# Output weights loaded together, the spectra's groups finished in steps, and the context's norm at the end of its stage

## The chip, the cores and the metric

The kernel runs on one core of a Trainium2 chip. Its time is the device time of one execution in microseconds, and a kernel's time is the median of its runs. Engines are PE (TensorE: matmuls and transposes), DVE (VectorE), ACT (ScalarE), POOL (GpSimd) and SP (SyncE, which issues nearly all transfers here). A transfer is issued by an instruction on SP, which first waits for whatever its buffer waits for; what stands behind it on SP waits as well.

## The reference, cut to what matters

Two layers over 1024 latent tokens of width 1024, with 256 context tokens ahead of them. Layer 0 is attention, layer 1 a recurrence beside a long convolution whose filters come out of a small network. All of it is f32; the kernel splits each f32 operand into a high and a low part and makes a product of three matmuls.

```python
def attn_layer(...):                     # layer 0
    ...
    y = jnp.concatenate([o_a * silu(ga), o_b * silu(gb)], axis=-1) @ w_out
    x = x + gate[:, None] * y
    if ctx_out:
        yc = jnp.concatenate([oa_c * silu(ga_c), ob_c * silu(gb_c)], axis=-1) @ w_out
        ctx = ctx + gate_c * yc

def rec_layer(...):                      # layer 1
    u = modulate(x, norm_g, shift[:, None], scale[:, None]) @ w_in
    uc = modulate(ctx, norm_g, shift_c, scale_c) @ w_in
    ...
    y_hy = hyena_operator(u_hy, hy_short, hyena_filters(...), hy_skip)

def modulate(x, gain, shift, scale):
    return rms_norm(x, gain) * (1 + scale) + shift

def fft_long_conv(z, kern, skip):
    kf = jnp.fft.rfft(kern, n=2 * L, axis=0)      # the filters' spectra
    ...
```

## The kernel before

**Order.** The program is written once, stage after stage, and a scheduler with a timeline model of its own then orders the instructions of each engine. Within `attention` PE is kept in the order of the program; the other engines are the scheduler's. So where an instruction stands on DVE, ACT, POOL and SP is not told by the source; the section on the change shows rows of that order.

**Attention (to 1083 us).** 80 units of two heads by 128 queries: 40 of dense attention (`units_b`), then 40 of `units_a`, four head pairs j with two context units and eight window units (ty, gi) each. `mix` weaves the scores of a unit with the transposes (`pt_ps`) and the output product of the unit before, and calls `next(self.fill)` between them: other work on PE, a slice at a time. A window unit takes the minimum of scores plus bias on DVE (`pn`, L700, L890), the exponentials on ACT (L695), and its bias from POOL (L881) out of a mask and a table (`namask`, `tt`), both loaded for it.

**The spectra (643 to 990 us)** are the first such fill: `hyena_kernels` makes 80 steps, for each of 4 filter blocks (half, o) eight steps of values and two transforms `dft` of six steps. A transform ends with four groups g: a combine (L1805, DVE for g = 0 and 3, POOL for 1 and 2), a multiply by the norm (L1806, DVE), the skip term (L1902, POOL) and the store to `HS` on SP. The tile `hs` has two buffers, and all four groups stand in the program right behind the last step.

**The output weights (990 to 1046 us).** At unit (2, 0, 3) `load_wo` loads `attn_w_out` in eight blocks of 512 KB through two raw tiles; each half block is cast on ACT (`wo_hi`, L192) and its rest taken on POOL (`wo_lo`, L196). From unit (3, 0, 1) the fill is `context_rows`: the output product of the context's two tiles (`c_ps`), whose first input is the load `m` (L957), cast to `m0h`.

**The output product (1083 to 1207 us).** `gemm2` first norms the two context tiles (rows of the modulation `mod` and the gain loaded there, L970 to L973; `norm_mod` L329 to L347: mean square on ACT, scale L339 on DVE, shift L340 on POOL except for tile 9, eight transposes `nm_ps`, a cast and a low part), then takes the latent tiles 2 to 9, 48 matmuls `g_ps` each, gate and residual (L986, L987), store of `X`, and the same norm. Behind it the context is stored (`XC`, L1027), its tiles are given up, and `gemm3` loads its weights `w_raw` (L365), from which ACT casts `w_hi`; `hyena`'s tables `hiv`, `hfw` and `hs` are loaded there too.

## Time and profile before

| | |
|---|---|
| median of 3 runs | 2482.05 us (2478.19 to 2484.31) |
| profiled execution | 2487.22 us, of it the span of the trace 2485.4 us |
| TensorE's granted clock, mean over the span | 0.938 |
| busy share of the span | PE 92%, its weight loads 76%, DVE 63%, ACT 47%, POOL 37% |
| transfers | 362 MB, mean 146 GB/s |
| chain that ended last, by engine | PE 27%, DVE 9%, DMA 3%, issue 2% |

All rows of the trace below are of the profiled execution; times in them are counted from the span's start. The clock's two levels are 1.2 and 2.4 GHz, so a mean of 0.83 in a stretch means that a third of it ran at the lower one.

### The profile page before, as it was taken

Reading aid. Unit: us, or ns where it says so; the run is one execution under the profiler, and the core shown is the slowest. Engines: PE = TensorE matmul, PEld = TensorE weight load, DVE = VectorE, ACT = ScalarE, POOL = GpSimd, SP = SyncE. Lnnn points to the kernel's source line nnn. Section 1 sums busy time; section 2 is a strip of 40 time slices with the busy share of each in tenths; the row PEclk is TensorE's granted clock in tenths of the full one; section 3 lists DMA queues with packets and bytes.
Section 4 is the critical chain, followed back from the end, with each engine's and each line's share of the span. In section 5 each row is a group of like instructions: output and inputs, shape, how many; then the busy total and the mean of one; then the engine's idle time right before and its main releaser. Section 6 shows DMA issues by size and latency. Waiting matters only on the chain. (4 is left out here: it accounts for less than half of the span.)

```text
span 2485.4 us, 45290 instructions
## 1 busy us (share of the span) xinstructions
PE 2275.4 (92%) x16647; PEld 1892.6 (76%) x16647; DVE 1568.8 (63%) x3175; ACT 1177.3 (47%) x2695; POOL 931.4 (37%) x959
## 2 busy tenths in 40 slices
PE   4999999999999989779899889999968999998997
PEld 3877888777878877668778778788757877887775
DVE  6255532368667867455486696457797776777425
ACT  5354434456556555532323221366435656665334
POOL 1253235201011654511033244224745464655512
PEclk8999999999999989889999999999858989999999
DMA  8433344682222766843454544574534343444522
GB/s 280 132 123 119 126 147 146 196 254 93 80 68 90 200 199 183 225 165 110 144 164 150 164 158 136 173 257 134 155 85 131 107 122 97 115 134 126 168 73 92
DMA packets 351428, 361.69 MB, mean 146 GB/s; under 512 B 83106, under 2 KB 283055, under 8 KB 350438
## 3 DMA queue, kind: packets, MB, share of 16 engines
q1 hardware_dynamic: 341894, 330.34, 43.5%
q10 hardware_dynamic: 9168, 24.25, 3.2%
q0 software_dynamic: 144, 4.19, 0.4%
q8 instruction: 132, 2.16, 0.4%
q14 instruction: 90, 0.74, 0.1%
HBM read 260.07 MB, written 100.10 MB: 145 GB/s over the span
## 5 line engine op out<-in xcount | busy, mean ns | idle before, releaser
L158 PE MATMUL g_ps<-xl,w_hi 128*128 128x512 f32 x1056 | 268.0, 399 | 1.0 <-ACT w_hi L192 1.0
L158 PEld LDWEIGHTS g_ps<-xl,w_hi 128*128 128x128 f32 x1056 | 198.9, 191 | 44.0 <-issue 1.9
L158 PE MATMUL s_ps<-k,q 128*128 128x256 f32 (+1 forms) x704 | 199.9, 381 | 7.6 <-DVE pn L700 4.3
L441 POOL TENSOR_TENSOR al_acc<-al_acc,al_t 128x512 f32<-128x512 f32 x98 | 129.0, 1316 | 185.6 <-ACT al_t L439 155.5
L196 DVE TENSOR_TENSOR w_lo<-w_raw,w_hi 128x256 fp32r<-128x256 f32 (+1 forms) x184 | 131.2, 769 | 86.6 <-PE g_ps L158 45.3
L187 ACT COPY pt<-pt_ps 128x512 f32<-128x512 f32 (+1 forms) x203 | 102.1, 506 | 139.3 <-PE pt_ps L161 133.7
L1586 DVE TENSOR_TENSOR tmp<-L,X 80x112 f32<-80x112 f32 (+25 forms) x279 | 136.4, 489 | 17.8 <-DMA L<-LD 8.9
L1588 DVE TENSOR_TENSOR X<-X,tmp 80x112 f32<-80x112 f32 (+25 forms) x279 | 140.6, 504 | 6.5
L158 PE MATMUL g_ps<-xl,w_lo 128*128 128x512 f32 x528 | 137.8, 395 | 0.0
L161 PE MATMUL pt_ps<-ident,p 128*128 128x128 f32 x704 | 118.1, 283 | 17.7 <-DVE pt L185 7.5
L158 PE MATMUL g_ps<-xhi,w_hi 128*128 128x512 f32 (+1 forms) x528 | 118.2, 366 | 8.9 <-DVE ac_res L283 4.7
L161 PEld LDWEIGHTS pt_ps<-ident,p 128*128 128x128 f32 x704 | 80.8, 141 | 52.9 <-DVE pt L185 14.8
L158 PEld LDWEIGHTS s_ps<-k,q 128*128 128x128 f32 x704 | 109.9, 200 | 14.6 <-DVE p L700 7.1
L695 ACT ACTIVATE p<-p,mn 128x1280 f32<-128x1280 f32 (+1 forms) x96 | 103.4, 1077 | 35.7 <-DVE p L700 35.5
L439 ACT ACTIVATE al_t<-al_w,condT 128x512 f32<-128x512 f32 x98 | 70.8, 722 | 101.7 <-POOL al_acc L441 60.9
L158 PE MATMUL g_ps<-xhi,w_lo 128*128 128x512 f32 (+1 forms) x528 | 118.2, 362 | 0.0
L881 POOL TENSOR_TENSOR bias<-namask,tt 128x384 f32<-128x384 f32 x64 | 67.5, 1055 | 125.9 <-DVE mn L890 52.0
L158 PEld LDWEIGHTS g_ps<-xl,w_lo 128*128 128x128 f32 x528 | 98.2, 188 | 21.1 <-issue 1.4
L158 PE MATMUL g_ps<-xlo,w_hi 128*128 128x512 f32 (+1 forms) x528 | 112.8, 356 | 0.0
L158 PEld LDWEIGHTS g_ps<-xhi,w_hi 128*128 128x128 f32 x528 | 90.0, 194 | 29.5 <-DVE qraw L549 5.4
L158 PE MATMUL g_ps<-AKR,BK 64*128 64x128 f32 (+1 forms) x640 | 91.1, 335 | 22.6 <-DVE AKR L1505 14.8
L158 PEld LDWEIGHTS g_ps<-xhi,w_lo 128*128 128x128 f32 x528 | 89.0, 189 | 18.9 <-issue 5.8
(438 smaller groups left out, 5869.4 us busy)
## 6 DMA issues: line engine op xcount, KB each, us to landing
w_raw<-rec_w_in SPq DMA_DIRECT2D x33, 512.0 KB
hfw<-FW SPq DMA_DIRECT2D x32, 512.0 KB
w_raw<-attn_w_in SPq DMA_DIRECT2D x13, 1024.0 KB
al_w<-rec_ada_w SPq DMA_DIRECT2D x48, 256.0 KB
tt<-TG SPq DMA_DIRECT2D x64, 192.0 KB
kkf<-KK SPq DMA_DIRECT2D x40, 256.0 KB
q<-qb SPq DMA_DIRECT2D x64, 128.0 KB
HS<-hs SPq DMA_DIRECT2D x32, 256.0 KB
```

The lines of the kernel that those rows point to most:

```text
L158: return self.keep(self.pe.matmul(*args, **kw))
L161: return self.keep(self.pe.transpose(*args, **kw))
L187: self.nc.scalar.copy(out=out, in_=in_)
L196: e.tensor_tensor(out=lo, in0=full, in1=hi.bitcast(F32), op=ALU.subtract)
L439: nc.scalar.activation(out=o, in_=wt, func=AF.Copy, scale=self.condT[:, k, ci:ci + 1])
L441: nc.gpsimd.tensor_tensor(out=t, in0=t, in1=o, op=ALU.add)
L695: self.nc.scalar.activation(out=p, in_=p, func=AF.Exp, bias=mn, scale=-1.0, accum_out=rs)
L881: nc.gpsimd.tensor_tensor(out=b, in0=mask, in1=tt, op=ALU.subtract)
L1586: nc.vector.tensor_tensor(out=tv, in0=L[:, s:s + 1, rt].to_broadcast([n, nj, nt]), in1=X[:, rj, s:s + 1].to_broadcast([n, nj, nt]), op=ALU ...
L1588: nc.vector.tensor_tensor(out=X[:, rj, rt], in0=X[:, rj, rt], in1=tv, op=ALU.subtract)
```

## The change

Three stages are rewritten.

1. The spectra: the four combines of a transform stand together at its end, POOL's two first; multiply, skip term and store of the groups go into a list, `self.later`, of which one entry is taken at each later step, the remainder at the end. `hs` has four buffers, `hskip` two.
2. The output weights: eight raw tiles, on buffers of the pool that later holds the tiles of the output product; their loads are issued together at unit (2, 0, 3). One block is split in each unit of (2, 1), in the two context units of j = 3, and in (3, 0, 0) and (3, 0, 1). The weights are sixteen tiles instead of two. ACT's casts are kept in the order of the program. `namask` has three buffers instead of four.
3. `norm_rows` loads the rows of the norm; the latent ones at (3, 0, 0). `gemm2` takes the latent tiles first and the context's norm last, with rows that reuse the buffers of the latent ones.

```diff
@@ attention, units_a
                     for slot in range(2):
                         z = slice(slot * 128, slot * 128 + 128)
+                        if j == 3:
+                            next(split)
...
                     if (j, ty, gi) == (2, 0, 3):
                         for _ in self.fill:
                             pass
-                        self.load_wo(pool)
+                        self.fill = iter(())
+                        split = self.load_wo()
+                        next(split)
+                    elif j == 2 and ty == 1 or (j, ty) == (3, 0) and gi < 2:
+                        next(split)
+                    if (j, ty, gi) == (3, 0, 0):
+                        self.mods0 = self.norm_rows(0)
                     if (j, ty, gi) == (3, 0, 1):
+                        assert next(split, None) is None
                         self.fill = self.context_rows(self.ap)
@@ window_unit
-        mask = pool.tile([128, 384], F32, name="namask", tag="namask", bufs=4)
+        mask = pool.tile([128, 384], F32, name="namask", tag="namask", bufs=3)
@@ load_wo
-        whi = p.tile([128, KT, D], F32R, name="wo_hi")
-        wlo = p.tile([128, KT, D], F32R, name="wo_lo")
+        self.wo = [[p.tile([128, D], F32R, name=f"wo{i}{k}") for k in range(KT)] for i in range(2)]
...
-        with self.tc.tile_pool(name="wo_raw", bufs=1, side="right", reuse_waits="tile") as rp:
-            raws = [rp.tile([128, D], F32, name=f"wo_raw{i}") for i in range(2)]
-            for k in range(KT):
-                raw = raws[k % 2]
-                nc.sync.dma_start(out=raw, in_=a["attn_w_out"][k * 128:(k + 1) * 128, :])
-                for z in (slice(0, 512), slice(512, 1024)):
-                    self.split(whi[:, k, z], wlo[:, k, z], raw[:, z])
-        self.wo = whi, wlo
+        raws = [self.m_pool.tile([128, D], F32, name="wo_raw", tag=t, bufs=1)
+                for t in ("mod1", "mod0", "xt", "mod2", "m0h", "m0l", "x_c0", "x_c1")]
+        for k in range(KT):
+            nc.sync.dma_start(out=raws[k], in_=a["attn_w_out"][k * 128:(k + 1) * 128, :])
+        yield
+        for k in range(KT):
+            hi, lo = self.wo[0][k], self.wo[1][k]
+            for z in (slice(0, 512), slice(512, 1024)):
+                self.tc.keep_in_program_order(nc.scalar.copy(out=hi[:, z], in_=raws[k][:, z]))
+                nc.gpsimd.tensor_tensor(out=lo[:, z], in0=raws[k][:, z], in1=hi[:, z].bitcast(F32), op=ALU.subtract)
+            yield
+
+    def norm_rows(self, ci):
+        nc, p = self.nc, self.m_pool
+        mods = {}
+        for kind in (1, 0):
+            t = mods[kind, ci] = p.tile([128, D], F32, name=f"mod{kind}", tag=f"mod{kind}", bufs=1)
+            nc.sync.dma_start(out=t, in_=self.AD[1][ci, kind * D:kind * D + D].partition_broadcast(128))
+        g = p.tile([128, D], F32, name="gain1", tag="xt", bufs=1)
+        nc.sync.dma_start(out=g, in_=self.a["rec_norm"].partition_broadcast(128))
+        nc.vector.scalar_tensor_tensor(out=mods[1, ci], in0=mods[1, ci], scalar=1.0, in1=g, op0=ALU.add, op1=ALU.mult)
+        return mods
@@ gemm2
-        for ci, tiles in ((1, range(2)), (0, range(2, 10))):
-            mods = {}
-            for kind, l in ((2, 0), (1, 1), (0, 1))[ci:]:
...
-            nc.vector.scalar_tensor_tensor(out=mods[1, ci], in0=mods[1, ci], scalar=1.0, in1=g, op0=ALU.add, op1=ALU.mult)
+        for ci, tiles in ((0, range(2, 10)), (1, range(2))):
+            mods = self.norm_rows(1) if ci else self.mods0
...
@@ dft
-        for g, x, y, op in ((0, "0+", "1+", ALU.add), (3, "0+", "1+", ALU.subtract), (1, "0-", "1-", ALU.add),
-                            (2, "0-", "1-", ALU.subtract)):
-            e = nc.vector if g in (0, 3) else nc.gpsimd
-            t = wp.tile([128, 2, W], F32, name="hs", tag="hs", bufs=2)
-            e.tensor_tensor(out=t, in0=half[x[0], x[1]], in1=half[y[0], y[1]], op=op)
-            nc.vector.tensor_tensor(out=t, in0=t, in1=nrm().unsqueeze(1).to_broadcast([128, 2, W]), op=ALU.mult)
-            put(g, t)
+        ts = {}
+        for g, x, y, op in ((1, "0-", "1-", ALU.add), (2, "0-", "1-", ALU.subtract), (0, "0+", "1+", ALU.add),
+                            (3, "0+", "1+", ALU.subtract)):
+            t = ts[g] = wp.tile([128, 2, W], F32, name="hs", tag="hs", bufs=4)
+            (nc.vector if g in (0, 3) else nc.gpsimd).tensor_tensor(out=t, in0=half[x[0], x[1]], in1=half[y[0], y[1]], op=op)
+
+        def finish(g):
+            nc.vector.tensor_tensor(out=ts[g], in0=ts[g], in1=nrm().unsqueeze(1).to_broadcast([128, 2, W]), op=ALU.mult)
+            put(g, ts[g])
+
+        self.later += [lambda g=g: finish(g) for g in (0, 3, 1, 2)]
@@ hyena_kernels
+        def now():
+            if self.later:
+                self.later.pop(0)()
...
+                        now()
                         yield
...
+            while self.later:
+                now()
```

What the scheduler makes of it, at the three places that the prediction speaks of. The lines are those of the kernel that the rows belong to; the semaphores that an instruction waits for stand in brackets, by the engine or transfer queue that raises them.

VectorE around the end of a transform (the third of eight), before: `d_h` are the transform's last sums, `hs` the groups, `hnrm` the norm; `fin`, `mst`, `ri`, `pn`, `pt` belong to the attention units.

```order
L1798 TENSOR_TENSOR d_h<-d_f,d_ps 128x512 [waits PE_49,Activation_49]
...
L1805 TENSOR_TENSOR hs<-d_h 128x512 [waits DVE_49]
L732 TENSOR_TENSOR fin<-rb_ps,g 128x128 [waits PE_49]
L1805 TENSOR_TENSOR hs<-d_h 128x512
...
L1806 TENSOR_TENSOR hs<-hs,hnrm 128x512 [waits DVE_49]
L733 TENSOR_TENSOR mst<-o_ps,fin 128x128 [waits DVE_49]
L1806 TENSOR_TENSOR hs<-hs,hnrm 128x512 [waits DVE_49]
...
L890 ISA pn,mn<-s_ps,bias,mn 128x384 [waits DVE_49,PE_49]
...
L1806 TENSOR_TENSOR hs<-hs,hnrm 128x512 [waits DMAHW3_49,Pool_49]
...
L890 ISA pn,mn<-s_ps,bias,mn 128x384 [waits DVE_49,PE_49]
...
L1806 TENSOR_TENSOR hs<-hs,hnrm 128x512 [waits DMAHW5_49,Pool_49]
```

The same place in the changed kernel:

```order
L1820 TENSOR_TENSOR d_h<-d_f,d_ps 128x512 [waits PE_49,Activation_49]
L725 RECIPROCAL ri<-rs 128x2 [waits Activation_49]
L1827 TENSOR_TENSOR hs<-d_h 128x512 [waits DMAHW3_49]
L1827 TENSOR_TENSOR hs<-d_h 128x512
L732 TENSOR_TENSOR fin<-rb_ps,g 128x128 [waits DMAHW5_49,PE_49]
L1830 TENSOR_TENSOR hs<-hs,hnrm 128x512 [waits DVE_49]
L1830 TENSOR_TENSOR hs<-hs,hnrm 128x512 [waits Pool_49]
L1830 TENSOR_TENSOR hs<-hs,hnrm 128x512 [waits DVE_49]
...
L733 TENSOR_TENSOR mst<-o_ps,fin 128x8x16 [waits DMAHW2_49,DVE_49]
...
L1830 TENSOR_TENSOR hs<-hs,hnrm 128x512 [waits Pool_49]
```

The two multiplies of POOL's groups stood behind the next step's work; now all four multiplies follow the two combines, and two of them wait for POOL.

SyncE from the first output weights to the context's first `m`, before; `mod_11527` is the context's gate, `x_c` its residual rows, `M` the store of attention's output.

```order
L922 DMA wo_raw_10752<-attn_w_out 128x1024 [waits DMAHW7_49]
L922 DMA wo_raw_10753<-attn_w_out 128x1024 [waits DMAHW0_49]
L846 DMA vw_11263<-VA 32x4x128 [waits DMAHW1_49]
...
L922 DMA wo_raw_10752<-attn_w_out 128x1024 [waits DMAHW5_49,Pool_49]
...
L922 DMA wo_raw_10753<-attn_w_out 128x1024 [waits DMAHW2_49,Pool_49]
...
L922 DMA wo_raw_10752<-attn_w_out 128x1024 [waits DMAHW3_49,Pool_49]
...
L933 DMA mod_11527<-AD_98 128x1024 [waits DMAHW5_49]
L938 DMA x_c_11535<-ctx 128x1024 [waits DMAHW6_49]
...
L922 DMA wo_raw_10753<-attn_w_out 128x1024 [waits DMAHW0_49,Pool_49]
...
L922 DMA wo_raw_10752<-attn_w_out 128x1024 [waits DMAHW7_49,Pool_49]
...
L957 DMA m_11529<-M_96 128x8x128 [waits DMAHW4_49]
...
L922 DMA wo_raw_10753<-attn_w_out 128x1024 [waits DMAHW0_49,Pool_49]
```

The same place in the changed kernel; `mod_11308`, `mod_11310` and `gain` are the latent norm's rows, `mod_11550` the context's gate:

```order
L888 DMA tt<-TG 128x1x384 [waits DMAHW1_49,Pool_49]
L931 DMA wo_raw<-attn_w_out 128x1024 [waits DMAHW2_49]
...
L931 DMA wo_raw<-attn_w_out 128x1024 [waits DMAHW1_49]
L833 DMA M_96<-mst 128x512 [waits DMAHW2_49,DVE_49]
L831 DMA g<-G_67 128x512 [waits DMAHW3_49]
...
L946 DMA mod_11308<-AD_99 128x1024 [waits DMAHW1_49,Pool_49]
...
L946 DMA mod_11310<-AD_99 128x1024 [waits DMAHW2_49,Pool_49]
...
L948 DMA gain_11312<-rec_norm 128x1024 [waits DMAHW4_49,Pool_49]
...
L958 DMA mod_11550<-AD_98 128x1024 [waits DMAHW3_49,Pool_49]
...
L963 DMA x_c_11558<-ctx 128x1024 [waits DMAHW5_49,Pool_49]
...
L963 DMA x_c_11859<-ctx 128x1024 [waits DMAHW1_49,Pool_49]
...
L982 DMA m_11552<-M_96 128x8x128 [waits DMAHW6_49]
```

All eight loads stand in a row (the first and the last are shown), and the load of `m` now has three rows of the norm and both context rows ahead of it, each of which waits for POOL.

SyncE at the end of the output product, before: `hiv`, `hfw` and `hs` are the convolution's tables and spectra. The context's store `XC` had gone out earlier in the stage.

```order
L989 DMA X_97<-xr 128x1024 [waits DMAHW2_49,DVE_49]
L989 DMA X_97<-xr 128x1024 [waits DMAHW6_49,DMAHW4_49,DVE_49]
L365 DMA w_raw<-rec_w_in 128x8x128 x2
L1916 DMA hiv<-k_idft 128x4096 [waits PE_49]
L1925 DMA hfw<-FW 128x1024 x2
L1953 DMA hs<-HS_5058 128x512
```

The same place in the changed kernel:

```order
L1011 DMA X_97<-xr 128x1024 [waits DMAHW0_49,DVE_49]
L946 DMA mod_12779<-AD_99 128x1024 [waits DVE_49]
L946 DMA mod_12781<-AD_99 128x1024 [waits DMAHW4_49,DVE_49,Pool_49]
L1952 DMA hiv<-k_idft 128x4096 [waits DVE_49,PE_49,Activation_49]
L1961 DMA hfw<-FW 128x1024 [waits PE_49]
...
L1989 DMA hs<-HS_5058 128x512
L1049 DMA XC<-xc_12071 128x2048 [waits DMAHW1_49,Activation_49]
L1989 DMA hs<-HS_5058 128x512 [waits DMAHW2_49]
L1049 DMA XC<-xc_12072 128x2048 [waits DMAHW3_49,DVE_49]
...
L365 DMA w_raw<-rec_w_in 128x8x128 [waits DMAHW6_49,DMAHW1_49]
L365 DMA w_raw<-rec_w_in 128x8x128 [waits DMAHW7_49]
```

The rows of the context's norm wait for DVE's last use of the latent ones; the stores of the context stand behind the tables, and the first load of `gemm3`'s weights behind them waits for one of the stores to have landed.

## Rows read from the trace of the kernel before

**Rows 1.** The page's first part: busy time of each engine, its share of the span, and the number of instructions.

```profile
PE 2275.4 (92%) x16647; PEld 1892.6 (76%) x16647; DVE 1568.8 (63%) x3175; ACT 1177.3 (47%) x2695; POOL 931.4 (37%) x959
```

**Rows 2.** Windows (start:end in us from the span's start): length, then busy us and instructions of PE, PE's weight loads, VectorE, ScalarE and GpSimd, then TensorE's granted clock as a share of full speed, the mean busy share of the DMA engines, and GB/s.

```profile
643.00:990.00 347.00, 320.24 (x2880) 278.11 (x2876) 262.12 (x711) 193.08 (x370) 123.50 (x115) 0.96 0.47 137
990.00:1020.00 30.00, 20.38 (x190) 16.49 (x186) 14.68 (x57) 15.48 (x36) 16.79 (x15) 0.87 0.86 237
1020.00:1040.00 20.00, 13.95 (x100) 11.78 (x101) 10.08 (x31) 12.28 (x26) 12.05 (x11) 0.76 0.99 262
990.00:1050.00 60.00, 44.33 (x355) 36.66 (x352) 28.83 (x103) 31.94 (x70) 34.85 (x31) 0.83 0.88 244
1094.00:1114.20 20.20, 7.16 (x27) 4.39 (x25) 15.10 (x18) 4.62 (x9) 8.71 (x6) 0.58 0.65 227
1198.20:1207.10 8.90, 1.95 (x9) 1.58 (x9) 5.79 (x15) 3.32 (x8) 0.00 (x0) 0.78 0.76 219
1207.00:1220.00 13.00, 12.91 (x51) 10.56 (x52) 3.14 (x9) 3.11 (x10) 0.00 (x0) 0.89 1.04 376
```

**Rows 3.** The view of waits, VectorE, 643 to 990 us: what waited for what, us in total, times, the longest.

```profile
DVE hs L1806 <- POOL hs L1805: 9.3, 5, 4.7
```

**Rows 4.** The timeline of VectorE between 886 and 970 us: start, length in us, line, operation, tiles, shapes, count, and in brackets the idle time before it with what ended that.

```profile
891.92 1.73 DVE L1806 TENSOR_TENSOR hs<-hs,hnrm 128x512 f32<-128x512 f32 x1 [4.74 <-POOL hs L1805]
...
894.69 0.69 DVE L1806 TENSOR_TENSOR hs<-hs,hnrm 128x512 f32<-128x512 f32 x1
...
967.04 1.77 DVE L1806 TENSOR_TENSOR hs<-hs,hnrm 128x512 f32<-128x512 f32 x1 [1.82 <-POOL hs L1805]
```

**Rows 5.** The timeline of GpSimd at 890 us, columns as before.

```profile
890.63 2.48 POOL L1805 TENSOR_TENSOR hs<-d_h 128x512 f32<-128x512 f32 x2 [4.91 <-DMA HS<-hs]
```

**Rows 6.** The view of waits, PE, 643 to 990 us.

```profile
PE s_ps L158 <- DVE pn L700: 4.3, 2, 4.0
PE pt_ps L161 <- ACT pn L695: 3.7, 3, 1.8
...
PE s_ps L158 <- DVE p L700: 2.4, 3, 1.8
PE d_ps L158 <- DVE d_h L1798: 2.2, 1, 2.2
```

**Rows 7.** Instructions of one tile or line over the whole span: line, engine, operation, tiles, count, then shortest/median/longest in ns, and the first and last start in us. SPq are the DMA issues on SyncE.

```profile
L196 POOL TENSOR_TENSOR wo_lo<-wo_raw,wo_hi x16: 1267/1274/1302, 999.2 to 1045.1; 128x512 fp32r<-128x512 f32 x16
L922 SPq DMA_DIRECT2D wo_raw<-attn_w_out x8: 333/377/520, 991.2 to 1033.9; - x8
...
L881 POOL TENSOR_TENSOR bias<-namask,tt x64: 992/1010/1466, 514.4 to 1063.0; 128x384 f32<-128x384 f32 x64
...
L973 DVE SCALAR_TENSOR_TENSOR mod<-mod,gain x2: 1208/1216/1224, 1094.8 to 1105.9; 128x1024 f32<-128x1024 f32 x2
...
L340 POOL TENSOR_TENSOR nm_h<-nm_h,mod x18: 1262/1472/1717, 1096.9 to 1192.3; 128x512 f32<-128x512 f32 x18
```

**Rows 8.** The view of waits, ScalarE, 985 to 1046 us.

```profile
ACT wo_hi L192 <- DMA wo_raw<-attn_w_out: 12.8, 6, 4.2
```

**Rows 9.** The view of waits, PE, 985 to 1050 us.

```profile
PE pt_ps L161 <- ACT pn L695: 12.9, 5, 4.7
```

**Rows 10.** The timeline of ScalarE from 996 to 1208 us.

```profile
998.49 1.14 ACT L192 CAST wo_hi<-wo_raw 128x512 fp32r<-128x512 f32 x2 [3.52 <-DMA wo_raw<-attn_w_out]
...
1037.34 1.04 ACT L192 CAST m0h<-m 128x1024 fp32r<-128x1024 f32 x1 [0.86 <-DMA m<-M]
...
1113.12 1.04 ACT L192 CAST m0h<-m 128x1024 fp32r<-128x1024 f32 x1 [5.26 <-DMA m<-M]
...
1136.26 1.05 ACT L192 CAST m0h<-m 128x1024 fp32r<-128x1024 f32 x1 [5.11 <-PE g_ps L158]
...
1171.77 1.05 ACT L192 CAST m0h<-m 128x1024 fp32r<-128x1024 f32 x1 [5.83 <-PE g_ps L158]
...
1206.63 1.63 ACT L192 CAST w_hi<-w_raw 128x256 fp32r<-128x256 f32 x5
```

**Rows 11.** The timeline of PE (matmuls and transposes) from 1036 to 1208 us.

```profile
1038.44 2.08 PE L158 MATMUL c_ps<-wo_hi,m0h 128*128 128x512 f32 x4 [0.88 <-ACT m0h L192]
...
1083.31 2.14 PE L158 MATMUL g_ps<-wo_hi,m0h 128*128 128x512 f32 x8
...
1092.55 1.98 PE L158 MATMUL g_ps<-wo_hi,m0l 128*128 128x512 f32 x8
...
1197.67 0.47 PE L158 MATMUL g_ps<-wo_hi,m0l 128*128 128x512 f32 x1
...
1207.09 1.22 PE L158 MATMUL g_ps<-xl,w_hi 128*128 128x512 f32 x2 [0.98 <-ACT w_hi L192]
```

**Rows 12.** The timeline of SyncE's DMA issues from 1029 to 1201 us.

```profile
1030.26 0.43 SPq L957 DMA_DIRECT2D m<-M  x1
...
1107.16 0.37 SPq L957 DMA_DIRECT2D m<-M  x1
...
1200.55 0.43 SPq L365 DMA_DIRECT2D w_raw<-rec_w_in  x1
```

**Rows 13.** The timeline of VectorE from 1083 to 1203 us.

```profile
1094.76 1.22 DVE L973 SCALAR_TENSOR_TENSOR mod<-mod,gain 128x1024 f32<-128x1024 f32 x1 [4.94 <-DMA gain<-rec_norm]
...
1202.01 1.41 DVE L339 SCALAR_TENSOR_TENSOR nm_h<-xr,nm_rs,mod 128x512 f32<-128x512 f32 x2
```

## What the change was expected to do

> **What bounds the kernel now.** Read the page's totals first, then the windows by stage, and last the waits inside the three stages that the change touches. TensorE is busy for 92% of the span [rows 1], so time can come only out of the holes in its work, and out of the stretches at the lower of its two clock levels (1.2 against 2.4 GHz) that stand beside the holes. The windows [rows 2] show where the holes are. From 643 to 990 us (attention with the filters' spectra woven in) PE is busy 320.24 of 347.00 us. From 990 to 1050, where the output weights come in, it is busy 44.33 of 60 at a clock of 0.83, and the DMA engines are at 0.88. At the opening of the output product, 1094.0 to 1114.2 holds only 7.16 us of PE work at clock 0.58; the end of that stage, 1198.2 to 1207.1, holds 1.95. The four parts of the change aim at these holes, and the last part makes one larger.
>
> **A, the spectra's groups.** What waits on them in 643 to 990: VectorE waited 9.3 us in 5 places for a GpSimd combine [rows 3], the longest 4.74 us, behind a GpSimd that had itself waited 4.91 us for a store of an older group, since only two buffers rotate [rows 4, 5]. PE passed some of it on: waits for pn, p and d_h of 4.3, 3.7, 2.4 and 2.2 us [rows 6], in all 12.6 us. The clock of 0.96 over 347 us [rows 2] means that some 28 us ran at half speed, which costs up to 14 us; the work of those stretches is not all PE's, and I give half of that, 7, to these waits. With four buffers and both GpSimd combines ahead, these waits go: 12.6 + 7 = 19.6 us at most. But the deferral reaches VectorE only in part. The order of the changed kernel (shown ahead) puts the two combines and all four multiplies within twelve instructions, where before two of the multiplies stood some fifteen further on. That is a burst of 6 x 0.69 = 4.1 us at the undisturbed duration, and 0.69 grows to 1.73 and 1.77 when GpSimd works beside it [rows 4], so it is 4 to 10 us long, ahead of the next scores' minima and of their exponentials. A burst that held PE up for 1.5 us in each of the 8 transforms would take back 12. I take -7. Ends: -16 (hardly any burst felt) and +6 (every burst costs PE about 3.2 us, near the 3.7 and 4.3 of [rows 6]).
> VectorE's multiply lasts 1.73 us while GpSimd's combines run and 0.69 just after them [rows 4, 5]. The Trainium skill, SBUF — State Buffer, "Who interferes with whom", states that a VectorE instruction with two SBUF inputs and a GpSimd instruction that reads SBUF contend for one port pair, which one of them holds for its whole length. The trace agrees by that pair of durations, and the rule speaks against this change, which sets the combines of both engines side by side; by it A would be nearer to +6 than to -7.
>
> **B, the output weights.** Before, two raw tiles rotate, so the eight loads go out between 991.2 and 1033.9 [rows 7], each after the split of an older one. ScalarE's casts stand in line with the softmax and wait 12.8 us for the loads, 6 times [rows 8], and PE waits 12.9 us for the pn behind them [rows 9]. Half speed costs up to (1 - 0.83) x 60 = 10 us here [rows 2]. So 23 us at most could come back. After, all eight loads go out together, and one wait remains: two casts stand in the unit after the issue, and a lone wait was 3.52 us [rows 10]. That would give about -18.
> What is late next is the context's product. Its matmul at 1038.44 waited for the cast of m [rows 11], whose load went out at 1030.26 [rows 12] and was waited for until 1037.34 [rows 10]. In the changed order the m load stands behind all eight raw loads, both rows of the latent norm with the gain, and both context rows, and each of those waits in SyncE's line for a GpSimd split (16 x 1.27 us beside biases of 1.01 us [rows 7]). The transfer engines were at 0.86 in 990 to 1020 and at 0.99 in 1020 to 1040, at 262 GB/s [rows 2]. Ahead of m come five more 512 KB pieces than before (the last raw tile, the two norm rows, the gain, the second context row): 5 x 2.0 = 10 us at that rate, 7 at the 376 GB/s that the gemm behind reached [rows 2]. The slack up to 1037 is 30 x 0.14 = 4. So the product may begin 3 to 6 us later than 1038, although the units ahead of it run sooner; nothing behind it can pass it on PE, whose order is the program's. I take 0, between -18 and +22 (the slower rival).
>
> **C, the opening of the output product.** The hole from 1094.0 to 1114.2 goes. Its first stop is the gain: VectorE stood 4.94 us until 1094.76 [rows 13]; then the context's norm goes through GpSimd at 1.47 us a half [rows 7], PE's transposes wait for it, and m of the next tile is late by 5.26 us [rows 10]. In the changed kernel the latent rows and gain are loaded during attention and the latent tiles come first. A tile in the steady part takes (1171.77 - 1136.26) / 3 = 11.84 us [rows 10]. The stage from 1083.31 to 1198.14 [rows 11] is 114.83 us; eight tiles at that pace, the last without another tile's transposes in it (11.2 us, as the first one's six groups of matmuls, 1083.31 to 1094.53 [rows 11]), are 7 x 11.84 + 11.2 = 94.1. So C is -21; ends -24 and -17.
>
> **D, the context's norm at the end.** Let T be the end of the last output matmul, 1198.14. Before, the last latent tile's norm and transposes lie between, and gemm3 begins at 1207.09 [rows 11], T + 9.0; its weights had been issued at 1200.55 [rows 12]. After, the context's rows reuse the buffers of the latent rows, so their loads go out once VectorE has read those for the last time: T + 5.3 (1202.01 + 1.41 [rows 13]). Landing 5 to 6 us, as the cast at 1113.12 waited for a load issued at 1107.16 [rows 10, 12]: T + 11. Scale by the gain, 1.2 us [rows 7], T + 12; first products 0.7, four GpSimd additions at 1.47: T + 18.8; the last transposes, cast and low part, 2 us more: T + 21. Only then can the store of the context leave, and the first weight load stands behind it in SyncE's line and waits until its first half has landed (the order shown ahead). That 1 MB shares the queue with a 2 MB table and 1.25 MB of other loads issued from T + 15: 4.3 MB at 376 GB/s are 11.5 us, so T + 27. Weights issued then need 6 us (1200.55 to 1206.63 [rows 10, 12]): T + 33. Against T + 9.0 that is +24. Ends +17 (store and loads each in 3 us) and +30.
>
> **E, the rest.** From about 1790 us the scheduler orders all engines otherwise, with the same work. I find no row that would give this a sign: 0, with 8 either way. The reduced mask buffers, 4 to 3, cost nothing while biases are made a unit ahead; if that cover fails, a bias of 1.01 us shows in a unit.
>
> **Sum.** -7 + 0 - 21 + 24 + 0 = -4. The profiled execution took 2487.2 us, so 2483.2, and it stood 5.2 above the median of the runs, 2482.05; so I forecast **2478**. A measurement of this kernel can tell about 0.3%, 7.4 us, from no change: the borders are 2474.6 and 2489.5. The forecast is no change that can be told; its own range is 2468 to 2488.
>
> **Rivals.**
> *Faster: the weights' stage runs through.* If the queue at depth moves the loads at 376 GB/s rather than 262, m is there as soon as the shortened units reach it, and B is -18: 2460. For it: the rate of 376 at 1207 to 1220, and 12.9 us of PE waits with one cause. Against it: share 0.99 in 1020 to 1040. Chance 0.25.
> *Slower: m comes late.* Place: SyncE's line in front of the m load; price: all eight raw tiles and the three norm pieces ahead of it instead of two raw tiles in flight, 11 x 2.0 = 22 us at 262 GB/s; it decides when the first context matmul begins after 1050, where the units have nothing left to cover it. 2500. For it: the full transfer engines; against it: much of this was loaded before m already. Chance 0.12.
> The Trainium skill, DMA: Bandwidth & Descriptors, "Queues, rings and completion order", says that each transfer engine takes the descriptors of one queue in the order issued, so that m's could not start ahead of what is in that line. No row here shows it; by the rule this rival would be likelier than I have it.
> *Slower: the bursts.* The multiplies are not spread, so A is +8 rather than -7: 2493. For it: 1.73 against 0.69 us. Against it: the bursts of before had two multiplies side by side and PE's waits were mostly at GpSimd's. Chance 0.13.
> Forecast 0.40; the other 0.10 is the order of the recurrent stage, both ways.
>
> **How the numbers follow.** Faster: 0.24 of the first rival, 0.14 of the forecast's lower part, 0.04 of the rest: 0.42. Slower: 0.11 + 0.09 of the two, 0.04 + 0.04: 0.28. Same: 0.30. The range takes in the first rival with its spread and the bursts, and leaves out most of a late m: 2455 to 2498.
>
> **What would show it.** C: no PE hole behind the first latent tile, last output matmul some 94 us after the first. D: a hole of 20 us or more before gemm3, with PE waiting for w_hi, which waits for a load. B: one ScalarE wait for a raw tile, and first context matmul at 1033 to 1043 (counted as before, less what A gave). A: no VectorE wait for GpSimd's combine over 1 us, but multiplies of over 1 us in a row. It is wrong if the first context matmul moves by over 10 us, if D's hole is under 12, or if the stage behind 1800 changes by over 8.

## The result

The changed kernel takes 2502.59 us (median of 4 runs, 2498.93 to 2507.42), the kernel before 2480.12 (4 runs). The ratio is 1.0091 with a 95% interval of 1.0063 to 1.012: **slower by 0.9%**, outside the forecast range of 2455 to 2498. The profiled execution took 2499.21 us, 12.0 more than the profiled one of before. Cut into stages by marks that both traces have, these 12 us are a sum of large terms of both signs:

| mark in the trace (us from the span's start) | before | changed | step |
|---|---|---|---|
| end of the attention unit under the last spectra | 981.2 | 996.8 | A +15.6 |
| first matmul of the context's product (`c_ps`) | 1038.4 | 1069.3 | B +15.3 |
| first matmul of the output product | 1083.3 | 1114.9 | +0.7 |
| last matmul of the output product | 1198.1 | 1208.7 | C -21.0 |
| first matmul of the projections (`gemm3`) | 1207.1 | 1247.3 | D +29.6 |
| end | 2485.4 | 2497.4 | E -28.2 |

**A.** VectorE in the changed kernel around the end of the third transform (start, length, line, operation, tiles, count, idle time before):

```profile
713.11 0.69 DVE L1820 TENSOR_TENSOR d_h<-d_f,d_ps 128x512 f32<-128x512 f32 x1 [1.01 <-PE d_ps L158]
713.71 2.36 DVE L1827 TENSOR_TENSOR hs<-d_h 128x512 f32<-128x512 f32 x2
716.00 3.49 DVE L1830 TENSOR_TENSOR hs<-hs,hnrm 128x512 f32<-128x512 f32 x3
719.41 0.28 DVE L732 TENSOR_TENSOR fin<-rb_ps,g 128x128 f32<-128x128 f32 x1
719.62 1.01 DVE L1830 TENSOR_TENSOR hs<-hs,hnrm 128x512 f32<-128x512 f32 x1
720.55 0.41 DVE L700 TENSOR_SCALAR_CACHE_REDUCE p<-s_ps 128x256 f32<-128x256 f32 x1
```

The six operations of the burst fill VectorE from 713.7 to 720.6, and the unit's minimum `p` comes only then. PE at that place:

```profile
721.66 1.12 PE L158 MATMUL o_ps<-pt,vb 128*64 128x128 f32 x8 [4.11 <-ACT p L695]
```

The unit with that wait takes 7.6 us where it took 2.9 before; in the unit behind it the kernel before is the slower one (9.7 against 6.4), and a lag of 5.2 us falls to 1.9. So this place shows how a burst acts, not what each costs. No wait for a GpSimd combine is left in this stretch: the waits of [rows 3] are gone, and the bursts cost more than they did. The stretch as a whole, before and changed (columns as in [rows 2]):

```profile
643.00:981.20 338.20, 313.04 (x2817) 272.27 (x2811) 254.16 (x689) 188.78 (x360) 116.06 (x108) 0.96 0.46 135
```

```profile
643.00:996.80 353.80, 317.76 (x2816) 276.67 (x2812) 262.51 (x679) 187.64 (x357) 126.60 (x106) 0.94 0.44 127
```

TensorE's idle time grew from 25.2 to 36.0 us; a second profile of each kernel has 25.0 and 37.0. So 11 to 12 us of A are holes that repeat. The other 5 are busy time at a lower mean clock, and in the second pair that part is -2.

The group rows of VectorE, 643 to 1000 us (busy, mean ns):

```profile
L1830 DVE TENSOR_TENSOR hs<-hs,hnrm 128x512 f32<-128x512 f32 x31 | 32.3, 1081 | 0.0
...
L1827 DVE TENSOR_TENSOR hs<-d_h 128x512 f32<-128x512 f32 x16 | 19.3, 1248 | 0.0
```

**B.** SyncE's issues of the output weights and of the context's loads:

```profile
1008.11 4.34 SPq L931 DMA_DIRECT2D wo_raw<-attn_w_out  x8
...
1053.01 0.38 SPq L963 DMA_DIRECT2D x_c<-ctx  x1
...
1055.45 0.33 SPq L963 DMA_DIRECT2D x_c<-ctx  x1
...
1059.70 0.38 SPq L982 DMA_DIRECT2D m<-M  x1
```

ScalarE and PE at the two ends of this stretch, which answer to [rows 10, 11]:

```profile
1014.02 1.14 ACT L936 CAST wo<-wo_raw 128x512 fp32r<-128x512 f32 x2 [5.41 <-issue]
...
1068.19 1.04 ACT L192 CAST m0h<-m 128x1024 fp32r<-128x1024 f32 x1 [10.00 <-DMA m<-M]
```

```profile
1069.29 2.08 PE L158 MATMUL c_ps<-wo,m0h 128*128 128x512 f32 x4 [12.96 <-ACT m0h L192]
```

Of the repeated waits for raw tiles [rows 8] one idle stretch of 5.4 us is left, as forecast; the view names nothing that ended it ("issue"), and the cast behind it comes 5.9 us after the first load left. But `m` leaves 51.6 us after the first raw tile, where it was 39.0, and PE stands 13 us for it.

**C and D.** Windows of the changed kernel (length, PE, PE's weight loads, VectorE, ScalarE, GpSimd, clock, share of the transfer engines, GB/s):

```profile
1115.00:1130.00 15.00, 15.00 (x66) 12.36 (x67) 6.41 (x10) 2.87 (x3) 0.00 (x0) 1.00 0.72 227
1130.00:1208.70 78.70, 78.70 (x374) 65.00 (x373) 41.05 (x64) 22.81 (x40) 20.33 (x14) 1.00 0.36 121
1208.70:1247.30 38.60, 6.87 (x29) 4.66 (x27) 15.28 (x27) 8.86 (x19) 6.13 (x4) 0.54 0.66 231
```

The output product runs without a hole at full clock, 93.8 us instead of 114.8. Behind it stands a hole of 38.6 instead of 9.0. SyncE and ScalarE in it:

```profile
1214.85 1.56 SPq L946 DMA_DIRECT2D mod<-AD  x2
1225.31 0.33 SPq L1952 DMA_DIRECT2D hiv<-k_idft  x1
...
1229.40 0.32 SPq L1049 DMA_DIRECT2D XC<-xc  x1
...
1240.49 8.63 SPq L365 DMA_DIRECT2D w_raw<-rec_w_in  x3
```

```profile
1246.86 1.32 ACT L192 CAST w_hi<-w_raw 128x256 fp32r<-128x256 f32 x4 [17.48 <-DMA w_raw<-rec_w_in]
```

With T as in the forecast, the end of the last output matmul: rows of the norm at T + 6, context's store at T + 20.7, weights at T + 31.8, their cast at T + 38. That is the chain of the forecast, with 11.1 us instead of 6 between store and weights. From the table's issue to the weights' the transfer engines were full:

```profile
1225.30:1240.50 15.20, 2.77 (x11) 1.57 (x9) 2.70 (x8) 1.76 (x3) 2.28 (x2) 0.50 0.93 338
```

**E.** The scan, from its first state matmul (`st_ps`) to the first matmul of the last projection (`fe_ps`), before and changed:

```profile
1874.10:2280.70 406.60, 385.90 (x4313) 323.79 (x4309) 303.88 (x707) 257.13 (x847) 227.22 (x321) 0.92 0.42 116
```

```profile
1911.50:2297.00 385.50, 373.01 (x4297) 310.37 (x4296) 292.72 (x709) 255.72 (x845) 229.97 (x320) 0.98 0.45 123
```

The same matmuls in another order: the scan is 21.1 of E's 28.2 us. PE's idle time in it fell from 20.7 to 12.5 us, and its busy time by 12.9 as the clock rose from 0.92 to 0.98.

### The profile page after: what moved, and what is told of

Same layout as the page of the kernel before. It is cut to its first block, busy times and chain, and to the rows that moved or that the text cites. A ratio compares the mean times of both kernels' runs of the same rounds, so it can differ in the third digit from the quotient of the medians.

```text
span 2497.4 us, 45285 instructions
## 1 busy us (share of the span) xinstructions
PE 2269.2 (91%) x16647; PEld 1885.8 (76%) x16647; DVE 1563.2 (63%) x3175; ACT 1177.2 (47%) x2695; POOL 945.7 (38%) x959
## 5 line engine op out<-in xcount | busy, mean ns | idle before, releaser
L1608 DVE TENSOR_TENSOR tmp<-L,X 80x112 f32<-80x112 f32 (+28 forms) x279 | 133.5, 478 | 24.8 <-DMA L<-LD 10.9
L1610 DVE TENSOR_TENSOR X<-X,tmp 80x112 f32<-80x112 f32 (+28 forms) x279 | 133.1, 477 | 6.1
L158 PEld LDWEIGHTS s_ps<-k,q 128*128 128x128 f32 x704 | 110.6, 201 | 15.3 <-DVE pn L700 7.9
L695 ACT ACTIVATE p<-p,mn 128x1280 f32<-128x1280 f32 (+1 forms) x96 | 103.4, 1077 | 38.3 <-DVE p L700 37.9
L158 PEld LDWEIGHTS g_ps<-xl,w_lo 128*128 128x128 f32 x528 | 98.3, 188 | 21.1 <-issue 1.4
L192 ACT CAST w_hi<-w_raw 128x256 fp32r<-128x256 f32 (+1 forms) x184 | 72.1, 463 | 77.9 <-PE g_ps L158 58.9
L158 PE MATMUL g_ps<-AKR,BK 64*128 64x128 f32 (+1 forms) x640 | 94.2, 324 | 12.8 <-DVE tmp L1608 7.3
```

The source lines that it names most:

```text
L158: return self.keep(self.pe.matmul(*args, **kw))
L192: nc.scalar.copy(out=hi, in_=full)
L695: self.nc.scalar.activation(out=p, in_=p, func=AF.Exp, bias=mn, scale=-1.0, accum_out=rs)
L1608: nc.vector.tensor_tensor(out=tv, in0=L[:, s:s + 1, rt].to_broadcast([n, nj, nt]), in1=X[:, rj, s:s + 1].to_broadcast([n, nj, nt]), op=ALU ...
L1610: nc.vector.tensor_tensor(out=X[:, rj, rt], in0=X[:, rj, rt], in1=tv, op=ALU.subtract)
```

## The experiments

All marks in one table, from one profiled execution of each kernel: end of the unit under the last spectra; from there to the first context matmul; the output product; from its end to the projections; from there to the end.

| kernel | A: unit | B: to `c_ps` | C: product | D: to `gemm3` | E: rest | median of runs |
|---|---|---|---|---|---|---|
| before | 981.2 | 57.2 | 114.8 | 9.0 | 1278.3 | 2480.1 |
| before_again | 984.1 | 55.5 | 115.7 | 8.9 | 1273.3 | one run |
| changed | 996.8 | 72.5 | 93.8 | 38.6 | 1250.1 | 2502.6 |
| changed_again | 994.0 | 71.6 | 94.4 | 38.4 | 1261.9 | one run |
| undo_spectra | 981.2 | 66.4 | 93.9 | 39.2 | 1253.4 | 2480.3 |
| undo_weights | 997.5 | 68.0 | 93.8 | 34.3 | 1271.6 | 2514.0 |
| context_norm_first | 992.5 | 71.6 | 95.8 | 16.6 | 1282.8 | 2497.8 |
| spread_multiplies | 970.0 | 69.9 | 93.8 | 38.2 | 1259.5 | 2476.2 |
| m_ahead | 993.6 | 66.9 | 93.9 | 38.1 | 1252.1 | 2493.1 |
| store_ahead_of_table | 993.2 | 69.0 | 93.8 | 37.4 | 1246.9 | 2502.1 |
| two_mended | 973.5 | 71.7 | 95.8 | 11.4 | 1270.0 | 2467.9 |
| three_mended | 974.5 | 66.3 | 95.9 | 11.3 | 1257.1 | 2455.4 |
| four_buffers | 976.5 | 60.8 | 114.6 | 9.0 | 1259.9 | 2466.2 |
| combines_on_vector | 988.7 | 71.2 | 93.8 | 38.3 | 1249.2 | one run |

The context's product between B and C took 43.7 to 45.6 us in all of them. The medians come from four sets of runs, in which the kernel before had 2480.1, 2481.7, 2479.9 and 2476.0; a ratio below is to the kernel before of the same set. E moves by up to 36 us from order to order, and a median can follow it rather than the edit: context_norm_first reaches the projections 25.9 us ahead of the changed kernel and has a median only 4.8 lower, and undo_weights is 8.6 ahead there and 11.4 slower. So the stages carry the argument, not the medians.

**undo_spectra**: `dft` and `hyena_kernels` of the kernel before in the changed one.

> The changed kernel with the spectra's groups as they were before (two buffers, each group finished where it is made). Theory 1 (the bursts of combines and multiplies on VectorE cost PE 15 us up to the last of the spectra and some 5 more in the unit behind): the unit that ended at 996.8 us ends at 981 to 984, the first context matmul begins at 1047 to 1052 instead of 1069.3, and the difference of 20 us is still there at the first matmul of the recurrent layer's projections (1227 instead of 1247). Theory 2 (the units are late for another reason, such as the three mask buffers): 994 or later. In the whole time the recurrent stage behind, whose order changes with every edit, may add or take up to 28 us, as it did between the two kernels.

Measured: 981.2, first context matmul 1047.6, projections 1225.8, that is 15.6, 21.7 and 21.5 us earlier than changed. Theory 1 holds in its numbers; the three mask buffers are no cause of A. That the 6 us behind the mark are the last burst's is not shown: eight issues fewer stand ahead of `m` in this run (52), and it leaves 45.8 us after the first raw tile instead of 51.6. 1.0002 (0.9981 to 1.0023) of before.

**undo_weights**

```diff
-        raws = [self.m_pool.tile([128, D], F32, name="wo_raw", tag=t, bufs=1)
-                for t in ("mod1", "mod0", "xt", "mod2", "m0h", "m0l", "x_c0", "x_c1")]
...
+            raw = self.m_pool.tile([128, D], F32, name="wo_raw", tag=("mod2", "x_c1")[k % 2], bufs=1)
```

> The changed kernel with the output weights loaded as before through two raw tiles (on buffers that the context's product needs only later), casts and splits where the scheduler puts them; the rest as changed. Theory 1 (the line of transfers on SyncE moves at one issue per 0.86 us, since each waits for the eighth before it, and m comes as many issues later as stand ahead of it: 60 in the changed kernel, 45 before, 55 here): first raw load to m's issue 47 us instead of 51.6, so the first context matmul some 4 to 6 us earlier, and ScalarE waits for raw tiles again (over 10 us in all). Theory 2 (the eight large loads in a row take the time): the first context matmul 57 to 60 us behind the last spectra's unit (996.8), as before, instead of 72.5, so 12 to 15 us earlier.

Measured: `m` left 47.3 us after the first raw tile, and the stretch from the spectra's unit is 68.0 instead of 72.5. ScalarE waited 12.8 us for raw tiles again. Theory 1, to a us in `m`'s issue; the first context matmul came 3.8 us earlier. The eight loads in a row are at most 4.5 of B's 15.3 us. 1.0162 (1.0111 to 1.0212) of before.

**context_norm_first**

```diff
-                        self.mods0 = self.norm_rows(0)
+                        self.mods0 = self.norm_rows(1)
...
-        for ci, tiles in ((0, range(2, 10)), (1, range(2))):
-            mods = self.norm_rows(1) if ci else self.mods0
+        for ci, tiles in ((1, range(2)), (0, range(2, 10))):
+            mods = self.mods0 if ci else self.norm_rows(0)
```

> The changed kernel with the context's norm first again, but on rows and gain that were loaded during attention, and the latent rows loaded behind it. Theory 1 (the changed order's last link, norm, store, then weights, costs 30 us at the end of the stage; the opening hole was the late gain and rows, not the order): no hole at the opening, last output matmul 93 to 98 us after the first (93.8 changed, 114.8 before), and 8 to 10 us from it to the projections' first matmul instead of 38.6: there 27 to 31 us earlier than the changed kernel. Theory 2 (the context's norm between the tiles makes the opening hole whatever was loaded): 110 to 115 us again, and a gain of 10 to 14 only.

Measured: output product 95.8, so the opening hole was the late rows and not the order. Behind it 16.6, not 8 to 10, because the table `hiv` had taken the place ahead of the weights. SyncE, then ScalarE:

```profile
1207.11 0.42 SPq L1952 DMA_DIRECT2D hiv<-k_idft  x1
1207.59 1.31 SPq L1961 DMA_DIRECT2D hfw<-FW  x2
1208.94 5.49 SPq L365 DMA_DIRECT2D w_raw<-rec_w_in  x2
```

```profile
1220.91 1.32 ACT L192 CAST w_hi<-w_raw 128x256 fp32r<-128x256 f32 x4 [7.61 <-DMA w_raw<-rec_w_in]
```

Weights issued at 1208.94 behind 3 MB are cast 12.0 us later; before, ahead of them, it was 6.1 [rows 10, 12]. 1.0075 (1.0042 to 1.0109) of before.

**spread_multiplies**

```diff
-            nc.vector.tensor_tensor(out=ts[g], in0=ts[g], in1=nrm()...
+            self.tc.keep_in_program_order(nc.vector.tensor_tensor(out=ts[g], in0=ts[g], in1=nrm()...
```

> The changed kernel with the four multiplies of each transform pinned to the place in VectorE's line that the program gives them, one per step, and the combines as changed. Theory 1 (the burst of six is what PE waits for): the unit that ended at 996.8 ends at 978 to 984, at or ahead of the kernel before, since the waits for GpSimd's combines are gone as well. Theory 2 (the combines of VectorE and GpSimd side by side are the cost, each at 1.25 us on VectorE instead of 0.69, and these stay): 990 or later.

Measured: 970.0, better than either bound: 24 to 27 us under the two profiles of the changed kernel and 11 to 14 under those of before. The combines are as slow as in the changed kernel:

```profile
L1830 DVE TENSOR_TENSOR hs<-hs,hnrm 128x512 f32<-128x512 f32 x32 | 30.8, 973 | 0.0
...
L1827 DVE TENSOR_TENSOR hs<-d_h 128x512 f32<-128x512 f32 x16 | 19.3, 1248 | 0.0
```

So the burst was what PE waited for (theory 2 had 990 or later), and the deferral does what it says only where VectorE's order is pinned. 0.9987 (0.9969 to 1.0005) of before, B and D still in it.

**m_ahead**: the load of `m` is written first at (3, 0, 1), and what must stand behind it is pinned.

```diff
+                        self.mc0 = self.load_m(0, self.m_pool)
+                        self.m_ctx = self.m_load
...
+            with self.tc.issue_after(self.m_ctx.ins):
+                nc.sync.dma_start(out=xt, in_=self.xsrc(tt))
```

> The changed kernel with one difference in SyncE's line: the load of the context's first m is written ahead of the masks and tables of the units from (3, 0, 2) on and of the context rows, and these are pinned behind it, so that 47 issues stand between the first raw load and m instead of 60. Theory 1 (the line moves one issue per 0.84 to 0.88 us whatever is in it, as in all six kernels so far): m goes out 40 to 41 us after the first raw load (51.6 in the changed kernel), and the first context matmul comes 8 to 12 us earlier, at 1057 to 1062. Theory 2 (m waits for the context's attention output or for the splits, not for the line): m at 1055 or later and the first context matmul at 1065 to 1070.

Measured: `m` left after 43.4 us, as SyncE first waited for the context's own store (1045.31), and the first context matmul came at 1060.5, 8.8 us earlier; 5.6 of these fall behind the spectra's unit. `m` was cast at 1052.84, though, 8 us ahead of the matmul. PE's one wait from 1048 to 1062:

```profile
PE pt_ps L161 <- ACT pn L695: 10.1, 1, 10.1
```

The tables put behind `m` are now what comes last; GpSimd, which makes the bias out of them, stood for one until 1054.66:

```profile
1054.66 2.28 POOL L895 TENSOR_TENSOR bias<-namask,tt 128x384 f32<-128x384 f32 x2 [11.90 <-DMA tt<-TG]
```

The line gives one transfer its place at another's cost. 1.0052 (1.0033 to 1.007) of before.

**store_ahead_of_table**

```diff
-                    nc.sync.dma_start(out=self.XC[p], in_=self.xc[p].bitcast(F32))
+                    self.xc_store = nc.sync.dma_start(out=self.XC[p], in_=self.xc[p].bitcast(F32))
...
+        with self.tc.issue_after(self.xc_store.ins):
+            nc.sync.dma_start(out=iv, in_=a["k_idft"])
```

> The changed kernel with the convolution's 2 MB table pinned behind the context's stores in SyncE's line (it stood ahead of them). Theory 1 (the store's landing took 11.1 us, 1229.4 to 1240.5, because the table and the other loads ahead of it shared the transfer engines; this is what the forecast's 6 us missed): the store lands in 6 to 8 us, but the weights now share the engines with the table, so from the last output matmul to the first of the projections 34 to 38 us instead of 38.6. Theory 2 (the store alone is that slow): 38 to 41.

Measured: 37.4. SyncE and ScalarE:

```profile
1221.28 0.32 SPq L1049 DMA_DIRECT2D XC<-xc  x1
...
1226.13 15.35 SPq L365 DMA_DIRECT2D w_raw<-rec_w_in  x4
```

```profile
1237.61 1.33 ACT L192 CAST w_hi<-w_raw 128x256 fp32r<-128x256 f32 x4 [16.36 <-DMA w_raw<-rec_w_in]
```

The store is through in 4.9 us instead of 11.1, so the forecast's 6 was the price of a store by itself; the weights, now sharing with the table, take 11.5 instead of 6.4. The table costs its 5 to 6 us wherever it stands ahead of the weights. 1.0077 (1.0051 to 1.0103) of before.

**two_mended**: `spread_multiplies` and `context_norm_first` together, and

```diff
+        self.first_w = self.last_load
...
+        with self.tc.issue_after(self.first_w.ins):
+            nc.sync.dma_start(out=iv, in_=a["k_idft"])
```

> The changed kernel with the multiplies spread one per step, the context's norm first on rows loaded during attention, and the convolution's 2 MB table behind the first two weight loads of the projections. Theory (each stage adds by itself): the last unit with spectra ends at 970, first context matmul 1040, first output matmul 1084, last 1180, first of the projections 1189 to 1191 (1207.1 before), and from there 1250 to 1283 us to the end, whatever the scheduler makes of it: 2441 to 2476 us in all. Rival: the mended stages interact (a shorter stage brings its loads onto those of the next), and the projections begin at 1197 or later.

Measured: 973.5 and 1045.2 at the first two marks, 95.8 and 11.4 us for product and hole, projections at 1197.4. That is 3.5 and 5.2 us late at the first two marks, 6.2 and 6.0 at the output product's ends, 6.4 at the projections, which is the rival's mark (1197 or later); most of it was there before the stage with the mended norm began. 0.994 of before (0.9916 to 0.9963).

**three_mended**: the same with `m_ahead`.

> The same as the one with two mended stages, and m ahead in SyncE's line (48 issues behind the first raw load instead of 59). Theory: the first context matmul at 1029 to 1033, the first of the projections at 1178 to 1183, and in all 2430 to 2468 us. Rival: the units in front now wait for their tables, which stand behind m, and the first context matmul's 10 us are given back before the first output matmul, which comes at 1081 or later.

Measured: first context matmul 1040.8, not 1029 to 1033; the rival was right that the units give it back, as in `m_ahead`. Projections at 1191.7, not 1178 to 1183; time 2455.42 us, **0.9889 of before (0.9865 to 0.9913)**: 1.1% faster than the kernel before, and faster than the changed one. Its output product and the hole behind it:

```profile
1084.50:1180.40 95.90, 95.90 (x456) 79.08 (x455) 56.36 (x86) 29.55 (x50) 26.60 (x18) 1.00 0.50 167
1180.40:1191.70 11.30, 2.36 (x13) 1.76 (x11) 6.67 (x15) 4.03 (x9) 0.00 (x0) 0.61 0.81 255
```

**four_buffers**: `bufs=2` to `bufs=4` for `hs` in the kernel before.

> The kernel before with four buffers instead of two for the groups of the spectra, and nothing else. Theory 1 (the forecast's upside was the waits for older stores, up to 19.6 us): VectorE no longer waits over 1 us for GpSimd's combine, and the unit that ended at 981.2 us ends at 968 to 974, as it did with the multiplies spread. Theory 2 (the waits were cheap; what the spread kernel gained came from the spreading): 978 to 982. In the whole time 0 to 12 us less than before.

Measured: 976.5, between the theories: 5 to 8 us under the two profiles of before. VectorE's wait for the combines, to set against [rows 3]:

```profile
DVE hs L1806 <- POOL hs L1805: 3.8, 3, 1.7
```

So four buffers alone were worth 5 to 8 us, and the kernel with the multiplies spread stands another 6.5 ahead, each in one profile. 0.9948 of before (0.9925 to 0.9972); most of it lies in the stage behind, which is also shorter in this profile (1259.9).

**combines_on_vector**

```diff
-            (nc.vector if g in (0, 3) else nc.gpsimd).tensor_tensor(out=t, in0=half...
+            nc.vector.tensor_tensor(out=t, in0=half...
```

> The changed kernel with all four combines of a transform on VectorE, so that no GpSimd combine runs beside it; the burst has eight operations instead of six. Theory 1 (the six operations were slow, 1.25 and 1.08 us on the mean, because GpSimd worked beside them): combines at 0.69 us, burst of 5.5 to 7 us instead of 8.2 to 9, the unit that ended at 996.8 ends at 988 to 993. Theory 2 (VectorE's number of operations in one go is the cost): 996 to 1003.

Measured: 988.7, with eight operations in the burst. The group rows:

```profile
L1830 DVE TENSOR_TENSOR hs<-hs,hnrm 128x512 f32<-128x512 f32 x32 | 26.6, 862 | 0.0
L1827 DVE TENSOR_TENSOR hs<-d_h 128x512 f32<-128x512 f32 x32 | 20.0, 687 | 0.2
```

A combine takes 0.69 us once none of GpSimd's combines runs beside it, against 1.25; the mark comes 5 to 8 us earlier, out of A's 10 to 16. The Trainium skill, SBUF — State Buffer, "Who interferes with whom", states that a VectorE instruction with two SBUF inputs contends with a GpSimd instruction that reads SBUF; the trace agrees by 687 against 1248 ns.

**before_again** and **changed_again**: no edit.

> The kernel before, profiled a second time. It tells how far one profile of the same instructions lies from the next. If the stages differ by order alone: last spectra unit 981, first context matmul 1038, first of the projections 1207, each within 4 us, and from there to the end 1278 within 4. If the stage behind moves by itself from run to run: there 1265 to 1280.

> The changed kernel, profiled a second time. If the stages differ by order alone: 997, 1069 and 1247 within 4 us at the three marks, and from the last to the end 1250 within 4. If the stage behind moves by itself from run to run: there 1250 to 1265, since the median of the runs lies 3.4 us above the profile that was shown and the highest 8.

Measured: all marks up to the projections repeat within 4.3 us, the terms C and D within 0.9. The rest does not: 1250.1 and 1261.9 for one and the same order. Its scan again, before and changed:

```profile
1876.60:2282.60 406.00, 385.83 (x4317) 323.49 (x4309) 303.63 (x705) 257.16 (x847) 227.18 (x323) 0.93 0.43 116
```

```profile
1906.60:2303.40 396.80, 384.03 (x4302) 320.14 (x4297) 297.73 (x712) 256.48 (x846) 226.52 (x321) 0.94 0.44 119
```

One order took 385.5 us at clock 0.98 and 396.8 at 0.94; PE's idle time in it was 12.5 and 12.8, so all 11 us are busy time at another clock. The kernel before repeats: 406.6 and 406.0, with 20.7 and 20.2 idle. So some 8 us of the scan's gain are holes that the new order doesn't have, in both pairs. Of E's -28.2 some 12 were the luck of one profile; -11 to -28 is what the four profiles give.

## Why the prediction was wrong

The chain of reasoning had the right places. Ahead of the projections two terms, A and B, were priced wrongly, both to the same side; behind them E was missed to the other.

- **A, the step "a burst that held PE up for 1.5 us in each of the 8 transforms would take back 12. I take -7".** Measured +10 to +16 over the four profiles. Pinning the multiplies alone gives back 24 to 27 us, so the bursts cost PE 3.0 to 3.4 us in each of the 8 transforms (an estimate, 24 and 27 over 8), twice what was taken; their length, 6.9 us in the one shown, was within the 4 to 10 of the forecast. The gross gain was set too high: without the bursts 11 to 14 us are to be had, and 5 to 8 from four buffers alone, not 19.6. The upper end of +6 priced a burst at 3.2, about what was measured, and fell short because it took off the same 19.6. That the deferral would not reach VectorE's order was read correctly.
- **B, the step "I take 0".** Measured +14 to +17 between the two marks. The places were right (ScalarE's waits went, `m` came late), and 13.0 us are PE's one wait for `m`. What failed is the count of what stood ahead of `m`: five more pieces of 512 KB, 10 us less 4 of slack. In the changed trace 60 issues and 14.0 MB stand there, against 45 issues and 9.4 MB (by the sizes of the issues): the five pieces and ten more of 64 to 256 KB (tables, masks, a gate, a store, a slice of values), which I did not count although they stood in the order. At the 0.86 us per issue that both lines ran at, fifteen more are 12.9 us, and `m` left 12.6 later; by bytes, 4.6 MB at 262 GB/s would be 17.5. SyncE's waits for GpSimd in that line, which the order had shown, came to 2.2 us. The rival of a late `m` had this mechanism, priced it at 22 us from the large pieces alone, and had too small a chance. What stays open: no run on the changed kernel brings this stretch under 66.3, so some 9 of B's 15 us have no run of their own, and with `m` ahead the units wait for their tables instead.
- **C** was forecast -21 and measured -21.0 and -21.3. The rows in hand, one full tile's period and the length of the stage, were enough.
- **D** was forecast +24 and measured +29.6, within its ends. The mis-sized term is the store's landing, 6 us against 11.1, beside a 2 MB table; store_ahead_of_table shows it at 4.9 without. The rate of 376 GB/s was nearly right (338 from the table's issue to the weights'); what moved in those 15.2 us was 5.1 MB and not 4.3, since the second half of the context's store and three more loads of the spectra went out in them too.
- **E** was 0 within 8; measured -28 and -11. No row gave it, and the bound was too narrow: the new order has some 8 us less of holes in the scan, and the scan's time goes with its clock, which differs from order to order and, for the changed kernel, from run to run.
- The sum hid this: +15.6 + 15.3 + 0.7 - 21.0 + 29.6 - 28.2 = +12.0; without E, which no step foresaw, it would have been +40. Against the forecast's -4 it is 16.0 too much: 22.6 from A, 15.3 from B, 5.6 from D and 0.7 from the context's product, less 28.2 from E. So the step that decides is A, and B next: the two slower rivals, held at 0.13 and 0.12, came together. The forecast named what would show it wrong, and two of the three signs came: the first context matmul moved by 30.9 us, and the stage behind by over 8. The remaining 8.6 us to 2502.6 are the step from profile to median: the forecast took off 5.2, by which the profiled execution of before stood above its median, and the changed kernel's stood 3.4 below its own.

## What to carry to other kernels

Work that is deferred in the source moves only on engines whose order follows the source; look at the order that the scheduler made, and pin it. To price a line of transfers, count every issue ahead of the one that matters, small ones included, and see what a transfer put first pushes back. A stage's last link (norm, store, then loads that reuse the store's memory) costs its whole length when nothing stands behind it, so put such a chain where matmuls cover it.

## What the runs showed of the hardware

- From the first raw tile to `m` SyncE issued 45 to 60 transfers in each of the fourteen traces, of 64 KB (`vw`) to 512 KB, at 0.80 to 0.93 us per issue. Each of the issues in the order's rows ahead of `m` waits on a transfer's semaphore, and in the trace each raises the one that the eighth before it raised; this is the program's order, with eight transfers in flight. SyncE's view of waits in the changed kernel, 1008 to 1062 us, has this at its top:

```profile
SPq L848 <- DMA wo_raw<-attn_w_out: 3.9, 4, 1.1
```

  The lines of that view that name a transfer add up to 20.7 us, those that name GpSimd or TensorE to 2.9. Whether the line is paid by the issue or by the byte these runs don't settle: the mean size was 208 to 238 KB in all of them, the same stretches moved 241 to 277 GB/s, and the transfer engines were busy for 0.88 to 0.93 of them. The count fits the pair better (12.9 us expected of fifteen issues, 12.6 measured). The number in flight was not varied.
- The scan's clock differed between two executions of the same instructions of the changed kernel, 0.98 and 0.94, and its length by 11 us. In the kernel before it was 0.92 and 0.93, and the length repeated within 0.6. The output product repeated within 0.9 us in both kernels.
- A VectorE combine of 128x512 took 0.69 us on the mean without a GpSimd combine beside it and 1.25 with one (combines_on_vector against the changed kernel).
